# Two fused transformer blocks on one core: six seams of the schedule re-laid at once

## Chip, cores and metric

The kernel runs on one core of one Trainium2 chip. The metric is the device time of one execution in microseconds (us), taken as the median of several runs. All times below are of the kernel before the change.

## Reference, cut to what matters

The input `x` is 1024 tokens by 1024 features, float32. Two blocks follow each other.

```python
def first_block(x, ...):
    h = rmsnorm(x, norm_g)                       # x * rsqrt(mean(x^2)) * g
    q, k, v, z_att, gb, gc, u, z_conv, g_att, g_conv = split(h @ w_in)
    att = chunked_rel_attention(q, k, v, rel_bias)         # 8 heads of 64
    y_att = (att * silu(z_att)) @ w_att_out
    y_conv = (gb * causal_conv3(gc * u) * silu(z_conv)) @ w_conv_out
    x = x + (sigmoid(g_att) * y_att + sigmoid(g_conv) * y_conv) @ w_out
    return rmsnorm(x, final_norm_g)

def second_block(h, mem, ...):
    hn = rmsnorm(h, g_mix)
    q_a, k_a, v_a, q_i, k_i, w_i, q_b, k_b, v_b = split(hn @ w_in_2)
    # index scores of 4 heads -> the 256 best keys of each query -> attention A over these
    # attention B: softmax(q1 k1) - lam * softmax(q2 k2), 4 heads, causal
    h = h + concat(out_a, out_b) @ w_out_2
    h = h + softmax(q k_mem) v_mem @ w_xo         # cross attention, 256 memory rows, 4 heads
    a, gate = split(rmsnorm(h, g_ffn) @ w_ffn_in)
    return h + (gelu(causal_conv3(a)) * gate) @ w_ffn_out  # 2816 wide
```

## The kernel before, in words

Matrices lie feature-major in SBUF as tiles of 128 partitions by 1024 columns. Each float32 operand is cut into a high and a low part by `split` (ScalarE writes `hi` at L130, VectorE writes `lo` = x - hi at L133), and a product of two such operands is three matmuls on TensorE, hi by hi, lo by hi and hi by lo (`mm3`, every matmul at L204). Weights come through `w` or `parts`: a load on SyncE's queue into a raw tile `wr`, then `wh` (ScalarE) and `wl` (VectorE). Finished tiles go back to HBM through `dspill` (a DMA issued by GpSimd, L174).

The work goes through stages that follow each other on TensorE:

- start: `x_load` loads the eight tiles of x, cuts them, and `qk_start` begins the first projections with k outermost; the first weights are whole 128x1024 tiles, and the vectors of gains (`gvec`), of biases (`bvec`) and the positions are loaded on ScalarE's queue.
- attention of the first block, then `gates`: for j = 0 to 3 two x tiles are normalised (`normed`), turned into `operands` for the seven-product scheme of the later projections, and the attention output projection (`wao`) runs into two S tiles of PSUM, which are then evicted in halves through `s2` and `s3`. For x tiles 4 to 7, `normed` scales on ScalarE and multiplies by the broadcast norm R on GpSimd (L1554); for tiles 0 to 3 it is one instruction on VectorE (L136).
- `mixer` of the second block: projections are made in groups of 196 or 256 columns for all eight token tiles (`tok_group`). The first group (196 columns: index key, shared key, shared value, index weights) takes two S tiles, its keys go through `rope` and are transposed (L874) to KI and KA, then follows the group of index queries (`w2i`, QI, transposes at L888), then the index scores. The 31 counting steps of the search for each row's 256th best score (`topk_step`) are woven into the groups that follow: three tiles are counted on ScalarE (Sign into `jka`, L130), three on VectorE, and VectorE then moves the threshold C (L136). The groups come in the order qb, kb, v, qa, two of each. `diff_prep` loads Q and K of a head pair and transposes them (L1163); it stands between the two qa groups.
- attention B and A, the cross attention's memory side and the cross attention itself (`cross`): for each of four heads, `cross_q` of the next head is woven into `cross_att` of this one; the last head has nothing to weave in. Then the output projection (`wxo`) in the order of tiles 0, 4, 1, 5, 2, 6, 3, 7 with `dense_full`, and `operands` of the feed-forward.
- feed-forward: 22 rounds of seven products P1 to P7 on half matrices (`product`), with `left_x` and `left_y` making the left operands. Round 0 (`begin(0)` and what follows) also sums the squares (`col_sums`, L204 into A), and broadcasts the norm (`put_R`).

PSUM has two S tiles of 1024 columns, two T tiles of 512 and one each of A and D. Inside stretches marked manual on TensorE its order is the order of the code; elsewhere a scheduler sets the order of each engine's instructions when the program is built. On the chip each engine takes its instructions in that order and stops at the first whose inputs are not there.

## Time and profile before

| what | value |
|---|---|
| runs shown, median of 3 (lowest to highest) | 2587.79 us (2441.83 to 12579.39) |
| the profiled execution's own time | 2432.4 us |
| its span | 2430.6 us |
| mean granted TensorE clock | 0.983 of full |

The three runs lie far apart. The rows below come from the profiled execution, so its own time is the one that they add up to; it is 9.4 us under the lowest of the three. The span is the time from the first to the last instruction that the profiler saw. Engines are PE (TensorE), PEld (its weight loads), DVE (VectorE), ACT (ScalarE), POOL (GpSimd), SP (SyncE). A timeline row reads: start in us, duration in us, engine, line, operation, output <- inputs with shapes, and in brackets how long the engine had stood idle before it and what released it.

### The profile page before, as it was taken

How to read it: one execution, taken by the hardware profiler on the slowest of the kernel's cores; microseconds unless marked ns; L12 is line 12 of the kernel's file. 1: busy time of each engine (PE TensorE's matmuls, PEld its weight loads, DVE VectorE, ACT ScalarE, POOL GpSimd, SP SyncE). 2: the span in 40 equal slices, each digit the busy share in tenths (PEclk: the TensorE clock that was granted, in tenths of full speed). 3: DMA queues.
4: the chain of work that ended last, by engine and by line, in shares of the span. 5: the costliest groups of instructions: out<-in, count | busy, mean ns of one | idle time of the engine just before them, and what ended most of it. 6: DMA issues, size and time to landing. Idle time of an engine off the chain costs nothing. (4 is left out here: it accounts for less than half of the span.)

```text
span 2430.6 us, 32666 instructions
## 1 busy us (share of the span) xinstructions
PE 2332.1 (96%) x12324; PEld 1975.2 (81%) x12324; DVE 1628.9 (67%) x2664; ACT 1230.8 (51%) x2064; POOL 240.8 (10%) x386
## 2 busy tenths in 40 slices
PE   8999999999999899978798999999999999999999
PEld 7887878888888899977686877887778888888887
DVE  5476786777565568668868875345678888774433
ACT  4455654444424346777676764344444554453231
POOL 0000020111101114231111110000000000000000
PEclk9999999999999899999899999999999999999999
DMA  4323265767648443346563225112322222225554
GB/s 143 102 68 115 72 224 218 271 222 253 230 166 340 152 122 117 127 121 209 181 202 104 84 73 196 65 64 92 121 78 79 79 87 83 88 85 177 186 172 145
DMA packets 111134, 347.24 MB, mean 143 GB/s; under 512 B 13568, under 2 KB 19072, under 8 KB 110976
## 3 DMA queue, kind: packets, MB, share of 16 engines
q1 hardware_dynamic: 84960, 252.11, 31.7%
q0 software_dynamic: 25584, 92.81, 10.0%
q8 instruction: 97, 1.59, 0.3%
q14 instruction: 61, 0.50, 0.1%
q10 hardware_dynamic: 432, 0.23, 0.1%
HBM read 223.46 MB, written 100.14 MB: 133 GB/s over the span
## 5 line engine op out<-in xcount | busy, mean ns | idle before, releaser
L204 PE MATMUL S<-U,wh 128*128 128x512 f32 x1792 | 582.7, 392 | 16.9 <-ACT U L130 8.5
L204 PEld LDWEIGHTS S<-U,wh 128*128 128x128 f32 x1792 | 338.2, 189 | 90.8 <-ACT U L130 8.5
L204 PE MATMUL S<-U,wl 128*128 128x512 f32 x896 | 350.9, 392 | 1.8 <-DVE wl L133 1.8
L204 PE MATMUL D<-U,wh 128*128 128x512 f32 x816 | 284.0, 400 | 0.7 <-ACT wh L130 0.4
L204 PE MATMUL S<-U,U 128*128 128x256 f32 (+6 forms) x1040 | 216.3, 334 | 13.5 <-DVE st L516 10.8
L204 PE MATMUL S<-U,PT 128*128 128x512 f32 x912 | 224.9, 395 | 0.9 <-ACT jkd L130 0.7
L130 ACT ACTIVATE wh<-wr 128x1024 fp32r<-128x1024 f32 (+1 forms) x89 | 87.4, 982 | 266.0 <-PE D L204 171.6
L204 PEld LDWEIGHTS S<-U,PT 128*128 128x128 f32 x912 | 171.0, 188 | 42.3 <-ACT jkd L130 1.7
L204 PEld LDWEIGHTS S<-U,wl 128*128 128x128 f32 x896 | 169.3, 189 | 39.2 <-DVE wl L133 3.2
L133 DVE TENSOR_TENSOR wl<-wr,wh 128x1024 fp32r<-128x1024 f32 (+1 forms) x89 | 101.6, 1142 | 148.0 <-ACT wh L130 148.0
L204 PEld LDWEIGHTS S<-U,U 128*128 128x128 f32 x1040 | 158.6, 197 | 29.5 <-DVE st L516 13.0
L204 PEld LDWEIGHTS D<-U,wh 128*128 128x128 f32 x816 | 153.1, 189 | 30.5 <-DVE U L133 1.1
L204 PE MATMUL D<-U,wl 128*128 128x512 f32 x408 | 162.3, 398 | 0.4 <-DVE wl L133 0.4
L204 PE MATMUL T<-U,wh 128*128 128x512 f32 x480 | 161.1, 390 | 0.0
L130 ACT ACTIVATE P<-P,st 128x640 f32<-128x640 f32 (+7 forms) x168 | 124.0, 739 | 39.6 <-DVE st L516 37.4
L204 PE MATMUL S<-wh,U 128*128 128x256 f32 x768 | 142.0, 287 | 0.0
L130 ACT ACTIVATE PT<-T 128x512 fp32r<-128x512 f32 (+4 forms) x208 | 110.9, 545 | 56.0 <-PE T L523 45.9
L174 POOL DMA_DIRECT2D sp<-P x102 | 54.3, 533 | 806.8 <-DVE P L133 549.5
L133 DVE TENSOR_TENSOR PT<-U,PT 128x1024 fp32r<-128x1024 f32 x74 | 67.8, 955 | 98.6 <-PE S L204 97.5
L133 DVE TENSOR_TENSOR P<-P,P 128x1024 f32<-128x1024 f32 (+3 forms) x105 | 119.7, 1148 | 18.6 <-ACT P L130 18.4
L133 DVE TENSOR_TENSOR U<-U,U 128x512 f32<-128x512 f32 (+3 forms) x146 | 114.8, 802 | 21.5 <-ACT U L130 20.8
L130 ACT ACTIVATE P<-P 128x1024 f32<-128x1024 f32 (+2 forms) x105 | 101.5, 968 | 47.8 <-DVE P L133 21.6
(303 smaller groups left out, 4754.4 us busy)
## 6 DMA issues: line engine op xcount, KB each, us to landing
sp<-P POOLq DMA_DIRECT2D x102, 512.0 KB, 3.5
U<-sp SPq DMA_DIRECT2D x93, 512.0 KB, 4.6
sp<-U POOLq DMA_DIRECT2D x69, 512.0 KB, 3.9
P<-sp SPq DMA_DIRECT2D x56, 512.0 KB, 4.5
U<-in_wf SPq DMA_DIRECT2D x43, 512.0 KB, 3.5
U<-in_w SPq DMA_DIRECT2D x30, 512.0 KB, 4.2
U<-U SPq DMA_DIRECT2D x116, 128.0 KB, 2.4
wh<-sp SPq DMA_DIRECT2D x24, 512.0 KB, 3.6
```

Source lines behind the costliest of these rows:

```text
L130: return self.nc.scalar.activation(out, in_, f, **kw)
L133: return self.nc.vector.tensor_tensor(out, a, b, op=op)
L174: self.nc.gpsimd.dma_start(dt, src)
L204: self.last = self.nc.tensor.matmul(out, l, r, start=start, stop=stop, skip_group_check=True)
```

## The change

Six places are changed.

1. First loads: the first two weight tiles come as a piece of 128 columns and the rest (`start_weights`), x tile 0 comes and is cut in two halves, and `bvec` and the positions move to SyncE's queue behind the x tiles.
2. `gates`: `normed` is the VectorE instruction for all eight tiles; the first `wao` group runs k = 0, k = 1, then k = 2 and 3 of one S tile and of the other.
3. First mixer group: the 196-column group goes into one S tile, D and A; `rope` writes into one U tile; the transposes of KI and KA come behind the 192 matmuls of the `w2i` group, which runs in two halves of the tokens; the column sums of the norm use T.
4. Order of the groups: qb, kb, qa, v; `diff_prep` stands behind the first v group.
5. `cross`: while the last head is made, the first output tile of `wxo` is begun in D and A from the parts that are there (`begun`), k = 0 to 5, and 6 and 7 behind it.
6. Entry of the feed-forward: the left operands of round 0 are made during the last `wxo` tile, four additions of them on GpSimd; the operands of tile 7 are made half by half (`last_operands`); the column sums stand behind P7 and the two halves of `put_R` apart, around P4.

```diff
 x_load
-            x = self.load(self.big("U"), self.I["xT"][k])
+            if k == 0:
+                next(ws[0][1])
+                for c in (slice(0, 512), slice(512, 1024)):
+                    self.load(x[:, c], self.I["xT"][k][:, c])
+                next(ws[1][1])
...
 first block
-        w = [self.w(I["w1"][0])]
-        hn = self.x_load(lambda: w.append(self.w(I["w1"][4], tag="P")))
+        w = [self.start_weights(z) for z in range(2)]
+        hn = self.x_load(w)
+        self.load(self.bvec, I["bv"].to_broadcast([128, NBV]))
+        self.load(self.posi, I["pos"])
...
 gates
         def normed(x, k):
-            if k < 4:
-                self.stt(x, x, self.gv("norm", k), R, OP.mult, OP.mult)
-            else:
-                self.act(x, x, scale=self.gv("norm", k))
-                nc.gpsimd.tensor_tensor(x, x, R, op=OP.mult)
+            self.stt(x, x, self.gv("norm", k), R, OP.mult, OP.mult)
...
-                for k in range(4):
-                    for z in range(2):
+                for ks in ((0,), (1,), (2, 3)):
+                    for z, k in [(z, k) for z in range(2) for k in ks]:
...
 tok_group
-        if small:
+        if small == "SDA":
+            b = [self.t("S", [128, 1024])] + [self.t(x, [128, 512]) for x in "DA"]
...
+        if halves:
+            order = [(kh, 4 * q + z, range(4)) for q in range(2) for kh in range(2) for z in range(4)]
...
 mixer, first group
-        for t0, nt, ps in self.tok_group(None, hn2, 196, ws=ws, mid={(2, 0): self.rms1, (2, 3): self.rms2}):
+        for t0, nt, ps in self.tok_group(None, hn2, 196, ws=ws, small="SDA", mid={(2, 0): self.rms1, (2, 3): self.rms2}):
...
+        QI = [self.big("U", F32R) for _ in range(4)]
+        ws = ahead()
+        views = self.tok_group(None, hn2, 256, ws=ws, halves=True)
+        for K, ko in zip((KI, KA), kos):
+            for half in range(2):
                 T = self.t("T", [128, 512])
                 for t in range(4):
-                    nc.tensor.transpose(T[0:64, t * 128:t * 128 + 128], ko[:, t, 0], self.ident)
+                    nc.tensor.transpose(T[0:64, t * 128:t * 128 + 128], ko[:, half * 4 + t], self.ident)
...
 mixer, order of the groups
-        for name, dest in (("qb", QB), ("kb", KB)):
+        for name, dest in (("qb", QB), ("kb", KB), ("qa", QA)):
...
             par += 1
+            if g == 0:
+                qk0 = self.diff_prep(0, QB[0], KB[0])
         VB[1] = [self.dspill(x) for x in VB[1]]
-        tab = self.rope_tab("qa")
-        rope_group("qa", QA, 0, tab)
-        qk0 = self.diff_prep(0, QB[0], KB[0])
-        rope_group("qa", QA, 1, tab)
...
 cross
+        def begun(ks):
+            if not part:
+                part.append(self.w(I["wxo"][0]))
+                part.extend(self.t(x, [128, 512]) for x in "DA")
+            for k in ks:
+                parts(k + 1)
...
+                    self.mm3(part[1 + half], part[0][0][:, c], part[0][1][:, c], res[k][0][:, sl], res[k][1][:, sl],
+                             k == 0, k == 7)
+                yield 1360
         for h in range(4):
-            fill = self.cross_q(h + 1, self.hn3, qs) if h < 3 else iter(())
-            drain(weave(self.cross_att(h, *qs[h], out), fill, 2.2))
+            fill = self.cross_q(h + 1, self.hn3, qs) if h < 3 else begun(range(6))
+            drain(weave(self.cross_att(h, *qs[h], out), fill, 2.2 if h < 3 else 0.6))
             drain(fill)
+        drain(begun(range(6, 8)))
...
                 wh, wl = self.w(I["wxo"][d])
+                self.left_x(0, I["wf1"][22], "wr")
+                self.left = self.left_y(0, I["wf1"][0], "P", True)
+                next(self.left)
...
+                last = self.last_operands(xg[3], x, ps)
+                self.B[3] = dict([next(last)])
...
 left_y(early=True)
+        tt = (lambda o, a, b, op: self.nc.gpsimd.tensor_tensor(o, a, b, op=op)) if early else self.tt
+        tt(s12[:, h[0]], y[:, h[0]], y[:, h[1]], OP.add)
+        tt(s12[:, h[1]], s12[:, h[0]], x[:, h[0]], OP.subtract)
+        if early:
+            tt(s4, x[:, h[1]], s12[:, h[1]], OP.subtract)
+            tt(y[:, h[0]], x[:, h[0]], y[:, h[0]], OP.subtract)
...
 feed-forward, round 0
-            if f == 0:
-                norm.append(self.mean_rsqrt(self.col_sums(R, 8), 8, 1.0 / 1024))
             self.product(c, A, "P6", False)
...
             if f == 0:
-                self.put_R(norm[0])
-            self.tt(a[:, h[1]], a[:, h[1]], R[:, h[1]], OP.mult)
+                norm.append(self.mean_rsqrt(self.col_sums(R, 8), 8, 1.0 / 1024))
+            else:
+                self.tt(a[:, h[1]], a[:, h[1]], R[:, h[1]], OP.mult)
             nxt = following()
+            if f == 0:
+                self.put_R(norm[0], (1,))
+                self.tt(a[:, h[1]], a[:, h[1]], R[:, h[1]], OP.mult)
             self.product(c, A, "P4", False)
+            if f == 0:
+                self.put_R(norm[0], (0,))
```

How the instructions stand is shown at three places. The first is TensorE between the first mixer group and the `w2i` group. Before, the four transposes of the first index keys (line L874) follow the last matmul of the 196-column group (S_7045) directly, ahead of the `w2i` group (S_7409):

```order
L204 MATMUL S_7045<-U_6989,U_6995 128x196
L204 MATMUL S_7045<-U_6990,U_6994 128x196
L874 MATMUL T_7291<-ident_69,P_7279 64x128 x4
L204 MATMUL S_7409<-wh_7034,U_6415 128x256
L204 MATMUL S_7409<-wh_7034,U_6416 128x256
```

Now the same transposes (L917, out of the U tile that `rope` wrote) stand at the end of the `w2i` group, behind its second S tile S_7393, and are followed by matmuls of the next group into D:

```order
L204 MATMUL S_7393<-wh_7046,U_7000 128x256
L204 MATMUL S_7393<-wl_7047,U_6999 128x256
L917 MATMUL T_7586<-ident_67,U_7037 64x128 x4
L917 MATMUL T_7595<-ident_67,U_7037 64x128 x4
L204 MATMUL D_7938<-U_7384,U_6420 128x256
L204 MATMUL D_7938<-U_7384,U_6421 128x256
```

So 192 matmuls (96 into each of S_7392 and S_7393) moved ahead of the transposes. The second place is TensorE at the head preparation of attention B. Before, the first transposes of Q (L1163) follow the last matmul of the first qa group, whose last tile is T_9656, and the second qa group (S_10025) follows them:

```order
L204 MATMUL T_9656<-U_9390,U_6995 128x256
L204 MATMUL T_9656<-U_9391,U_6994 128x256
L1163 MATMUL T_9975<-ident_69,U_9973 128x128 x4
L204 MATMUL S_10025<-wh_9645,U_6415 128x256
L204 MATMUL S_10025<-wh_9645,U_6416 128x256
```

Now the first v group stands there (last tile T_9723), and the transposes (L1202) come eight matmuls into the second v group (S_10064), two of them together:

```order
L204 MATMUL S_10064<-wl_9713,U_6504 128x256
L204 MATMUL S_10064<-wh_9712,U_6592 128x256
L204 MATMUL S_10064<-wh_9712,U_6593 128x256
L1202 MATMUL T_10012<-ident_67,U_10010 128x128 x4
L1202 MATMUL T_10023<-ident_67,U_10010 128x128 x4
L204 MATMUL S_10064<-wl_9713,U_6592 128x256
```

The transposes moved by eight matmuls, from behind a qa group to behind a v group. What ScalarE does for that v group's tiles is the third place; the rows that read D, A and T are the scaled copies of the group's tiles, `jka` are the counts of the search, three to a step:

```order
L130 ACTIVATE jka_111,cnt_7897<-U_7698,C_7895 128x768
L130 ACTIVATE jka_111,cnt_7897<-U_7699,C_7895 128x896
L130 ACTIVATE U_9710<-A_9721,r_7198 128x256 x2
L130 ACTIVATE jka_111,cnt_7897<-U_7700,C_7895 128x1024
L130 ACTIVATE jka_111,cnt_7897<-U_7698,C_7895 128x768
L130 ACTIVATE U_9711<-T_9722,r_7198 128x256
L130 ACTIVATE jka_111,cnt_7897<-U_7699,C_7895 128x896
L130 ACTIVATE U_9711<-T_9722,r_7198 128x256
L130 ACTIVATE jka_111,cnt_7897<-U_7700,C_7895 128x1024
L130 ACTIVATE U_9711<-T_9723,r_7198 128x256 x2
L130 ACTIVATE jka_111,cnt_7897<-U_7698,C_7895 128x768
L130 ACTIVATE U_10004<-T_10012 128x512
```

Before, at the same place, the copies of the qa group's tiles and the counts alternate in the same way:

```order
L130 ACTIVATE jka_113,cnt_7872<-U_7673,C_7870 128x768
L130 ACTIVATE P_9907<-T_9655,r_7191 128x256
L130 ACTIVATE jka_113,cnt_7872<-U_7674,C_7870 128x896
L130 ACTIVATE P_9907<-T_9655,r_7191 128x256
L130 ACTIVATE jka_113,cnt_7872<-U_7675,C_7870 128x1024
L130 ACTIVATE PT_9912<-P_9907 128x512
L130 ACTIVATE P_9935<-T_9656,r_7191 128x256
L130 ACTIVATE jka_113,cnt_7872<-U_7673,C_7870 128x768
L130 ACTIVATE P_9935<-T_9656,r_7191 128x256
```

The copies moved from the rope path (P and PT tiles) to plain copies into U, and the counts still stand between them.

## Rows read from the trace of the kernel before

**Rows 1.** Page, part 1: busy time, share of the span, instructions of each engine.

```profile
PE 2332.1 (96%) x12324; PEld 1975.2 (81%) x12324; DVE 1628.9 (67%) x2664; ACT 1230.8 (51%) x2064; POOL 240.8 (10%) x386
```

**Rows 2.** Windows: stretch, us, busy PE, PEld, DVE, ACT, POOL, clock, DMA, GB/s.

```profile
0.00:45.00 45.00, 34.59 (x160) 29.09 (x161) 26.56 (x36) 25.46 (x27) 3.50 (x41) 0.92 0.41 146
320.00:362.00 42.00, 37.62 (x155) 29.94 (x154) 35.67 (x40) 27.64 (x37) 14.65 (x4) 0.96 0.54 189
805.00:885.00 80.00, 72.42 (x557) 70.55 (x556) 36.00 (x85) 22.71 (x52) 11.95 (x17) 0.91 0.43 132
1045.00:1100.00 55.00, 35.86 (x274) 34.85 (x273) 41.07 (x106) 37.86 (x75) 22.19 (x31) 0.85 0.52 161
1100.00:1340.00 240.00, 209.79 (x1395) 182.40 (x1395) 190.49 (x482) 167.93 (x456) 33.67 (x44) 0.96 0.54 166
1640.00:1665.00 25.00, 19.76 (x96) 16.35 (x96) 13.24 (x20) 13.91 (x30) 1.64 (x1) 0.80 0.11 39
1750.00:1780.00 30.00, 24.14 (x105) 19.06 (x105) 19.37 (x25) 14.13 (x17) 2.56 (x2) 0.89 0.29 99
```

**Rows 3.** Timeline, the first 19 us.

```profile
4.93 0.17 DVE L133 TENSOR_TENSOR fgm<-gvec 128x8 f32<-128x8 f32 x1 [3.89 <-DMA gvec<-in_gv]
7.29 1.15 ACT L130 ACTIVATE U<-U,gvec 128x1024 fp32r<-128x1024 f32 x1 [1.49 <-DMA U<-in_xT]
8.49 0.79 PE L204 MATMUL S<-U,wh 128*128 128x512 f32 x1 [8.49 <-ACT U L130]
10.06 8.81 ACT L130 ACTIVATE U<-U,gvec 128x1024 fp32r<-128x1024 f32 x7 [0.20 <-DMA U<-in_xT]
```

**Rows 4.** Timeline of the gates' entry, 318 to 358 us.

```profile
320.65 1.28 DVE L136 SCALAR_TENSOR_TENSOR P<-P,gvec,R 128x1024 f32<-128x1024 f32 x1
327.36 2.39 POOL L1554 TENSOR_TENSOR P<-P,R 128x1024 f32<-128x1024 f32 x1 [3.18 <-ACT P L130]
328.26 2.57 DVE L133 TENSOR_TENSOR wl<-wr,wh 128x1024 fp32r<-128x1024 f32 x1 [1.01 <-ACT wh L130]
330.75 1.21 DVE L133 TENSOR_TENSOR U<-PT,U 128x1024 fp32r<-128x1024 f32 x1
349.47 6.39 POOL L1554 TENSOR_TENSOR P<-P,R 128x1024 f32<-128x1024 f32 x1 [8.64 <-issue]
357.97 0.50 PE L204 MATMUL S<-U,wh 128*128 128x512 f32 x1 [2.17 <-ACT jkd L130]
```

**Rows 5.** Timeline of the first mixer group, TensorE, 840 to 883 us.

```profile
840.14 1.06 PE L874 MATMUL T<-ident,P 128*64 128x128 f32 x4 [4.32 <-DVE P L133]
882.79 2.08 PE L204 MATMUL S<-U,U 128*128 128x512 f32 x8 [0.39 <-DMA U<-PT]
```

**Rows 6.** Timeline of attention B's entry, 1045 to 1100 us.

```profile
1046.04 0.94 ACT L130 ACTIVATE jka<-U,C 128x768 int8<-128x768 f32 x1 [0.56 <-DVE C L136]
1050.08 0.94 ACT L130 ACTIVATE jka<-U,C 128x768 int8<-128x768 f32 x1 [0.56 <-DVE C L136]
1060.55 1.12 PE L1163 MATMUL T<-ident,U 128*128 128x128 f32 x4 [10.80 <-ACT P L130]
1078.87 1.06 PE L1163 MATMUL T<-ident,U 128*128 128x128 f32 x8 [2.59 <-DMA U<-sp]
1096.69 0.58 PE L204 MATMUL D<-wh,U 128*128 128x256 f32 x1 [4.82 <-DMA U<-sp]
1099.06 0.40 ACT L130 ACTIVATE P<-P,st 128x128 f32<-128x128 f32 x1 [2.70 <-DVE st L516]
```

**Rows 7.** Timeline of the last cross head, 1640 to 1650 us.

```profile
1640.49 0.17 DVE L133 TENSOR_TENSOR st<-A,r 128x8 f32<-128x8 f32 x1 [1.96 <-PE A L204]
1648.32 1.94 PE L523 MATMUL T<-ident,P 128*128 128x128 f32 x8 [3.21 <-DVE P L133]
```

**Rows 8.** Timeline of the feed-forward's entry, TensorE, 1755 to 1762 us.

```profile
1755.99 1.95 PE L204 MATMUL A<-ones,R 128*128 128x1 f32 x16 [1.24 <-DVE R L133]
1761.35 0.80 PE L204 MATMUL S<-U,wh 128*128 128x512 f32 x1 [3.41 <-ACT wh L130]
```

More of the change, by code (lines that the diff above doesn't have):

```diff
@@ L527, in transposed, with put_R @@
         return PT
-    def put_R(self, r):
-        for half in range(2):
+    def put_R(self, r, halves=(0, 1)):
+        for half in halves:
             ps = self.t("T", [128, 512])
@@ L549, in x_load @@
             if k == 0:
-                between()
+                for z, n in ((1, 1), (0, 2), (1, 2)):
+                    for _ in range(n):
+                        next(ws[z][1], None)
         self.gate0 = his[GATE]
@@ L854, in mixer @@
         VA = self.big("U", F32R)
-        todo = [("w2i",)] + [(n, g) for n in ("w2q", "w2k", "w2v", "w2a") for g in range(2)]
+        todo = [("w2i",)] + [(n, g) for n in ("w2q", "w2k", "w2a", "w2v") for g in range(2)]
         ready = [self.first]
@@ L862, in ahead @@
             return ready.pop(0)
+        kos = self.big("U").rearrange("p (z t d) -> p z t d", z=2, t=8)
+        kos = [kos[:, z] for z in range(2)]
         ws = ahead()
[L865 removed]
+        for t0, nt, ps in self.tok_group(None, hn2, 196, ws=ws, small="SDA", mid={(2, 0): self.rms1, (2, 3): self.rms2}):
             self.v_split(ps[:, :, 128:192], t0, nt, VA.rearrange("p (t s d) -> p t s d", t=8, s=2)[:, t0:t0 + nt])
@@ L879, in mixer @@
         kas, vas = [self.dspill(k.bitcast(F32)) for k in KA], self.dspill(VA.bitcast(F32))
-        QI = [self.big("U", F32R) for _ in range(4)]
-        ws = ahead()
-        for t0, nt, ps in self.tok_group(None, hn2, 256, ws=ws):
+        for t0, nt, ps in views:
             qo = self.big("P")
@@ L1466, in rest @@
         def rest():
-            self.B[3].update(ops[3])
+            self.B[3].update(last)
             self.add_sq(acc, x, False)
@@ L1496, in operands, with last_operands, pair, put @@
                 yield n, (hi[:, c], lo[:, c])
+    def last_operands(self, x, y, ps):
+        h = [slice(0, 512), slice(512, 1024)]
+        u = self.big("U", F32R)
+        self.split(u[:, h[0]], u[:, h[1]], x[:, h[0]])
+        yield "11", (u[:, h[0]], u[:, h[1]])
+        def pair():
+            return self.big("U", F32R), self.big("U", F32R)
+        def put(v, hl, c, name):
+            self.split(hl[0][:, c], hl[1][:, c], v[:, c])
+            return name, (hl[0][:, c], hl[1][:, c])
+        z, zs = self.big("P"), pair()
+        for c in h:
+            self.tt(y[:, c], y[:, c], ps[:, c], OP.add)
+            self.act(z[:, c], y[:, c], scale=self.gv("ffn", 7))
+        yield put(z, zs, h[0], "21")
+        one, two = self.big("PT"), self.big("PT")
+        self.tt(one[:, h[0]], x[:, h[1]], x[:, h[0]], OP.subtract)
+        self.tt(two[:, h[0]], z[:, h[1]], one[:, h[0]], OP.subtract)
+        twos = pair()
+        yield put(two, twos, h[0], "T2")
+        ones = pair()
+        yield put(one, ones, h[0], "T1")
+        self.tt(one[:, h[1]], z[:, h[1]], x[:, h[1]], OP.subtract)
+        yield put(one, ones, h[1], "T3")
+        self.tt(two[:, h[1]], z[:, h[0]], two[:, h[0]], OP.subtract)
+        yield put(two, twos, h[1], "N4")
+        yield put(z, zs, h[1], "22")
     def left_x(self, f, ap, tag="U"):
@@ L1777, in ffn @@
             self.rest()
-            drain(self.left_y(0, I["wf1"][0]))
+            drain(self.left)
             for f in range(22):
```

107 lines of the change are left out of this document (68 added, 39 removed).

## Prediction

> **What bounds the kernel now.** I read the busy times first: TensorE works 2332.1 of 2430.6 us [rows 1], so all its waits together are 98.5 us, and an edit that takes no matmul away can gain only from these waits and from matmuls that run at a lowered clock. Then I read the windows of the places that the six edits touch, where the idle time is the stretch less the busy time of TensorE [rows 2]: start 45.00 − 34.59 = 10.4; gates 42.00 − 37.62 = 4.4; first mixer group 7.6; entry of attention B 19.1; last cross head 5.2; feed-forward entry 5.9. Together 52.6 us. The attention stretch behind the entry, 1100 to 1340, holds another 30.2, which no edit aims at. The clock column of the same rows is below 1.00 in each: if I charge the busy time of each with what is missing from full clock (34.59 × 0.08, 37.62 × 0.04, 72.42 × 0.09, 35.86 × 0.15, 19.76 × 0.20, 24.14 × 0.11), I get 2.8 + 1.5 + 6.5 + 5.4 + 4.0 + 2.7 = 22.9 us. That is an upper bound, since part of the lowered clock belongs to waits that stay. So the six places hold at most 52.6 + 22.9 = 75.5 us, 3.1% of the time; what each edit gets of it is read from the timelines, by asking what ends the wait and what is late next.
>
> The sums are made against the profiled execution's own 2432.4 us (span 2430.6 and 1.8 around it). The median of the runs shown, 2587.79, comes from three values far apart; the lowest, 2441.83, is 9.4 above the profiled one. I take the profiled one as the kernel's time.
>
> **First loads in pieces.** TensorE's first matmul is at 8.49; it waits for the cut of x tile 0 on ScalarE, which takes 1.15 from 7.29, after waiting for the tile's load [rows 3]. Ahead of it on SyncE's queue stood a whole weight tile; now a piece of 128 columns and half of x stand there (64 and 256 KB, where 1024 KB came before). The gain vector that the cut needs is there at 4.93 [rows 3], and that DMA is not moved, so a half-wide cut of some 0.6 (half of 1.15) can start at about 5.1 and the first matmul at about 5.7: 2.8 earlier. What is late next is x tile 1, cut from 10.06 on [rows 3]; twelve matmuls of 512 columns from 5.7 at 0.43 (512 columns at the lower of the clock's levels, 1.2 GHz) end near 10.8, and its cut ends at about 11.2 (10.06 + 1.15), with its low part behind it: a wait of about 0.7 comes back. 2.8 − 0.7 = 2.1, I take 2; bounds 1 and 3. The bias and position loads move past the x tiles on SyncE's queue; the rows show no use of them before the start's end, so I cost that at nothing, within the lower bound.
>
> **Gate norms on VectorE.** Removed: four GpSimd multiplies (2.39 to 6.39, in all 14.65 in this stretch) and four ScalarE scalings. Added: four VectorE instructions like the one of 1.28 at 320.65 [rows 4], 5.1 us. VectorE is busy 35.67 of 42.00 [rows 2], so 40.8 must fit. It gets something back: while GpSimd multiplies from 327.36 to 329.75, a VectorE subtraction begun at 328.26 takes 2.57, where the same size takes 1.21 at 330.75; 1.4 saved. The GpSimd multiply that runs among back-to-back VectorE work takes 6.39 [rows 4]. So VectorE ends at about 39.4 of 42 us: it still fits, with little room. The waits (idle 4.4, one of them the 2.17 at 357.97) are for what the S tiles' eviction and the late operands release, and the reordered first group finishes its first S tile 12 matmuls earlier. All 4.4 and some of the 1.5 of clock give 5 to 6; I take 5. Bounds 2 (VectorE late by up to 2 at the end, and no clock back) and 6.5.
>
> The same rows weigh a rule. The Trainium skill, page "SBUF — State Buffer", section "Who interferes with whom", says that a VectorE instruction with two SBUF inputs contends with a GpSimd instruction that reads SBUF, that the lock is on their one shared port pair, and that issue order decides who waits. The trace agrees: 329.75 + 1.21 = 330.96, and the subtraction ended at 330.83. By that rule this edit gains also what the waiting cost, but the four GpSimd additions of the feed-forward's entry, below, would bring the waiting back there.
>
> **First mixer group.** Before, TensorE stops 4.32 at 840.14 for the key transposes, because `rope` of 196-column tiles on VectorE is not finished; now 192 matmuls stand in between, and VectorE, busy 36.00 of 80.00 [rows 2], has the time. No matmul is added, and the work ahead of the index scores is the same, so these start earlier by the waits that go: the 7.6 of the stretch less the 0.39 in front of the scores [rows 5], 7.2, which puts the scores near 875.5 where 882.79 stood. I take 7 (waits alone, with any clock gained set against a new small wait). Low: the second half of `w2i` must still be roped and transposed before the scores with less behind it; if the last transposes wait 4, 3 is left. High: 9, with 2 of the 6.5 of clock.
>
> **Value groups last.** Before, three waits make 10.80 + 2.59 + 4.82 = 18.2 of the 19.1 [rows 6]. The first is for a T tile of PSUM that ScalarE copies late, because the copies stand among the counts of the search. After the change the transposes need T tiles that are released by the copies of T_9722 and T_9723, and between the group's first copies and these stand eight counts, 2.67 steps. A step takes 1050.08 − 1046.04 = 4.04 [rows 6], so 10.8; the eight matmuls ahead cover 1.7 (256 columns each, 0.21 at 1.2 GHz). 9.1 us of wait remain there. The other two waits are for loads from HBM (Q and K of the pair, and the memory weights); I let half of 7.4 remain, 3.7. So 18.2 − 9.1 − 3.7 = 5.4. Against that stands the end of this stretch: the first exponential at 1099.06 follows counting steps whose number (17) the edit does not change, and those are a chain of ScalarE and VectorE, not of TensorE. Filling work that TensorE does earlier is then missing behind it. I take 4. Bounds: 13 (most waits and the 5.4 of clock go) and −4 (the chain is untouched, and the memory work moved ahead is missing as fill in 1100 to 1340).
>
> **Last cross head filled.** From the row sums at 1640.49 to the transposes at 1648.32 the softmax of the last head takes 7.8, of which TensorE waits 3.21 [rows 7]; the stretch idles 5.2 and its clock is 0.80. Now the 48 matmuls of the first output tile are there to be spread, and in the built order 12 of them stand between the row sums and the last scores: at 0.21 to 0.43 each (512 columns at either clock) 2.6 to 5.1 us beside a wait of 3.2. But the parts of the output have to be cut first by ScalarE and VectorE, which are on the chain too, and later waits of the head have less fill. I leave 2 of the 5.2 and half of the 4.0 of clock: 3.2 + 2 = 5. Bounds 1 and 8. The matmuls are the same ones, so nothing is added; the eviction of D and A is two half-wide additions instead of one.
>
> **Feed-forward entry.** Waits 1.24 for the squares and 3.41 for `wh` [rows 8], 5.9 in all, and 2.7 of clock (the matmul at 1761.35 took 0.80). The left operands now come during the last projection, and column sums and norm move behind P7. What is late next are the right operands: `last_operands` is a chain of splits on ScalarE and subtractions on VectorE, half by half, that cannot start before the last projection ends. I let 3.5 of the wait and 2 of the clock stay: 8.6 − 5.5 = 3. GpSimd's four additions lie beside the last projection; at half of 2.39 each they are 4.8 us, covered. If they hold up VectorE as at 328.26, two collisions of 1.4 come on the path, and with the splits unchanged the gain is −1, the lower bound; the upper is 7.
>
> **Sum.** 2 + 5 + 7 + 4 + 5 + 3 = 26, and 2432.4 − 26 = 2406. All lower bounds: 1 + 2 + 3 − 4 + 1 − 1 = 2, so 2430; all upper bounds: 3 + 6.5 + 9 + 13 + 8 + 7 = 46.5, so 2386.
>
> **Rivals.**
> *The chains take it back.* Attention B's entry is bound by the counting steps and the feed-forward's by the splits, so these two give nothing or a little less: with 0 and −1, and 3 for the cross head, 2 + 5 + 7 + 0 + 3 − 1 = 16 and 2416. For it speaks that ScalarE's counts stand between the copies just as before; against it, that two of the three waits at the entry were for loads.
> *Nearly all of it goes.* The waits vanish where fill stands: 2386 by the upper bounds. Against it, each wait has a chain behind it that is not shortened. Only here does the time fall by over 2%.
> *Slower, through the attention stretch.* The work that fills attention B's entry now is missing in 1100 to 1340, where ScalarE and VectorE (167.93 and 190.49 of 240.00) feed TensorE. If the waits there multiply so that the clock falls from 0.96 to the 0.80 of the cross head's stretch, its 209.79 us become 209.79 × 0.96 / 0.80 = 251.7, 42 more; with the other five edits' 22, 2432.4 − 22 + 42 = 2452. It decides from a clock of about 0.87 on (209.79 × 0.96 / 0.87 = 231.5, the 22 gone). Against it: only 18 us of waits could move there, and 30.2 of them cost it 0.04 so far.
> *The change does not do what it says.* The fills could stand in the queue at places where they don't meet the waits, at the cross head above all; then the mixer's and the gates' gain alone remain: 2 + 5 + 7 = 14, 2418; this lies beside the first rival.
>
> **Chances.** The forecast 0.52; the chains take it back, or fills miss, 0.30; nearly all goes 0.12; slower than before 0.06. A measurement of this kernel can tell about 2% from no change, 48.6 us. Faster by that needs under 2384, beyond the upper bounds: half of the third case and a little for runs that scatter, 0.09; slower by that needs over 2481, beyond the slower case: 0.03; the rest is within. The range goes from 2388, leaving out the best of the third case, to 2438, which takes in the lower bounds' 2430 and most of the 9.4 by which a run can lie above the profiled one.
>
> **What would show it.** In the new profile: first matmul near 5.7; no GpSimd multiply in the gates, and VectorE done before TensorE needs its weights; index scores some 14 us earlier than before (2 + 5 + 7); at the first head transposes behind the v group one wait of 8 to 10 us, and the first exponential some 18 us earlier than 1099.06; transposes of the last cross head with a wait under 2; at the feed-forward's entry waits of 3 to 4 in all. The prediction is wrong if the transposes wait longer than the 10.80 of before, if the stretch behind the entry idles over 40, or if the four additions on GpSimd last over 3 us and VectorE's instructions beside them grow with them.

## Result and the profile after

The changed kernel takes 2409.69 us (median of four executions, 2408.14 to 2414.48), a ratio of 0.9887 to the kernel before, 95% interval 0.9863 to 0.9912: some 27 us less. Two of the three runs of before that were shown first had been disturbed; its later executions lie between 2430.27 and 2445.14, so the profiled 2432.4 is near their lower end. Against that one execution the gain is 22.7 us. Run again beside it on two other occasions, the same changed kernel gave 0.9890 (0.9870 to 0.9909) and 0.9891 (0.9873 to 0.9908). The profiled execution after is 2414.48, the slowest of its four, 17.9 under the profiled one of before; where two executions of one kernel come to differ by 6 us is seen in the table below.

Page, part 1, of the changed kernel, against [rows 1]:

```profile
PE 2335.0 (97%) x12324; PEld 1977.2 (82%) x12324; DVE 1632.2 (68%) x2682; ACT 1228.5 (51%) x2068; POOL 234.7 (10%) x388
```

TensorE does the same 12324 matmuls. The windows that answer to [rows 2], moved along with what each place had gained (columns as there: us, busy PE, PEld, DVE, ACT, POOL, clock, DMA, GB/s):

```profile
0.00:45.00 45.00, 36.66 (x158) 30.29 (x159) 26.80 (x38) 25.92 (x30) 3.50 (x41) 0.89 0.42 146
317.00:359.00 42.00, 41.25 (x179) 33.51 (x179) 40.89 (x47) 25.16 (x34) 0.00 (x0) 1.00 0.69 239
801.00:881.00 80.00, 75.23 (x572) 73.26 (x570) 38.06 (x98) 24.36 (x54) 12.53 (x19) 0.91 0.43 132
1039.00:1094.00 55.00, 43.87 (x320) 42.32 (x319) 35.89 (x116) 49.65 (x103) 4.06 (x14) 0.84 0.61 190
1094.00:1334.00 240.00, 207.94 (x1349) 180.11 (x1349) 187.07 (x467) 164.62 (x444) 33.07 (x43) 0.94 0.52 157
1633.00:1658.00 25.00, 22.95 (x128) 19.19 (x127) 13.97 (x21) 14.75 (x31) 1.64 (x1) 1.00 0.19 64
1734.00:1764.00 30.00, 27.22 (x121) 21.26 (x120) 24.67 (x35) 15.85 (x23) 2.60 (x2) 0.94 0.27 88
```

A window less the busy time of TensorE is what it waits. The gates wait 0.75 and the cross head 2.05 (4.4 and 5.2 before), both at the full clock. The start waits 2 us less, at a lower clock. The mixer still waits 4.8, attention B's entry 11.1 (7.6 and 19.1 before), and the stretch behind it 32.1 where it was 30.2. No experiment below undoes the filling of the last cross head; that its matmuls now stand in the waits of [rows 7] is read from TensorE's timeline, in which these waits are left:

```profile
1641.49 1.07 PE L529 MATMUL T<-ident,P 128*128 128x128 f32 x8 [0.66 <-DVE P L133]
1648.24 0.50 PE L204 MATMUL D<-U,wh 128*128 128x512 f32 x1 [1.40 <-ACT U L130]
```

Since the numbered order of the matmuls is the same in all kernels outside the changed places, the time between two equally numbered matmuls measures a place by itself. The table gives, from the trace of one execution of each kernel, the time of matmul 241 (end of the start), and the times from matmul 1741 to 2041 (gates), 3841 to 4621 (mixer to behind the index scores), 5701 to 7441 (attention B's entry to the end of attention), 8821 to 9121 (cross) and 9301 to 9661 (feed-forward's entry). The first four rows are the two kernels of the forecast and two repeats of the changed one; the other names are the experiments below.

```
kernel        start   gates   mixer  attention  cross  feed-forward
before        54.70   73.52  119.60   306.31    65.98   88.49
after         54.86   68.02  118.18   306.19    59.05   84.97
again         55.39   67.96  115.09   309.64    59.05   85.00
again2        57.21   67.75  112.62   306.14    59.05   85.00
no_start      54.67   67.95  114.78   305.63    59.03   84.96
no_mix        54.83   67.99  120.66   304.49    59.03   84.95
no_val        55.61   67.35  116.55   310.42    59.02   84.93
gpsimd_mul    57.19   72.41  115.76   304.74    59.03   84.97
start3        57.65   67.32  117.28   302.89    59.03   84.99
qi_queue      54.70   67.33  113.94   306.67    59.02   84.96
sums_early    57.47   67.35  115.13   307.23    59.02   92.03
left_dve      56.87   67.40  116.40   303.65    59.02   83.99
qi_pool       54.15   67.86  112.72   305.44    59.00   84.97
q_free        53.55   67.44  112.02   317.69    59.04   84.95
best          54.80   67.43  113.13   302.19    59.04   84.00
best2         55.97   67.69  111.42   318.26    59.03   83.98
best3         55.01   67.28  112.52   305.39    59.05   84.00
```

Three columns repeat within 0.8 us wherever their code is the same (gates, cross, feed-forward); start, mixer and attention scatter by 4 to 7 for identical code. So the pair before and after alone would have misjudged the mixer (1.4 won) and attention (0.1 won); with all kernels that have the new code there unaltered, the mixer is 115.8 on average (after, again, again2, no_start, no_val, gpsimd_mul, start3, sums_early, left_dve) against 119.6 and 120.7 with the old, and attention 305.4 (the thirteen without no_val, q_free and best2) against 306.3 and 310.4. The mixer's two old values lie above all nine new ones. Those of attention don't: the thirteen go from 302.2 to 309.6, with the old 306.3 among them.

### The profile page after: what moved, and what is told of

Read it like the earlier page. It is cut to its first block, busy times and chain, and to the rows that moved or that the text cites. A ratio compares the mean times of both kernels' runs of the same rounds, so it can differ in the third digit from the quotient of the medians.

```text
span 2412.7 us, 32693 instructions
## 1 busy us (share of the span) xinstructions
PE 2335.0 (97%) x12324; PEld 1977.2 (82%) x12324; DVE 1632.2 (68%) x2682; ACT 1228.5 (51%) x2068; POOL 234.7 (10%) x388
## 5 line engine op out<-in xcount | busy, mean ns | idle before, releaser
L204 PE MATMUL S<-U,wh 128*128 128x512 f32 x1768 | 575.3, 392 | 7.6 <-ACT U L130 6.0
L204 PEld LDWEIGHTS S<-U,wh 128*128 128x128 f32 x1768 | 333.3, 189 | 80.2 <-ACT U L130 6.4
L204 PE MATMUL D<-U,wh 128*128 128x512 f32 x832 | 290.5, 400 | 3.8 <-ACT U L130 2.6
L204 PE MATMUL S<-U,U 128*128 128x256 f32 (+6 forms) x944 | 207.6, 342 | 18.8 <-DVE st L522 12.7
L130 ACT ACTIVATE wh<-wr 128x1024 fp32r<-128x1024 f32 (+2 forms) x90 | 87.6, 973 | 263.4 <-PE D L204 171.5
L133 DVE TENSOR_TENSOR wl<-wr,wh 128x1024 fp32r<-128x1024 f32 (+2 forms) x90 | 100.4, 1116 | 148.6 <-ACT wh L130 148.5
L204 PEld LDWEIGHTS S<-U,U 128*128 128x128 f32 x944 | 148.9, 199 | 36.2 <-DVE st L522 14.7
L204 PE MATMUL A<-U,wh 128*128 128x512 f32 x384 | 131.4, 390 | 0.0
```

What stands on the lines that cost most here:

```text
L130: return self.nc.scalar.activation(out, in_, f, **kw)
L133: return self.nc.vector.tensor_tensor(out, a, b, op=op)
L204: self.last = self.nc.tensor.matmul(out, l, r, start=start, stop=stop, skip_group_check=True)
```

## Experiments

**The first loads** (no_start): change 1 undone. Of each edit the lines that matter are shown; three dots stand for the rest.

```diff
-        w = [self.start_weights(z) for z in range(2)]
-        hn = self.x_load(w)
+        w = [self.w(I["w1"][0])]
+        hn = self.x_load(lambda: w.append(self.w(I["w1"][4], tag="P")))
...
```

> The changed kernel with the first loads as before (whole weight tiles, x tile 0 whole, biases and positions on ScalarE's queue). Theory 1, what is won at the first matmul is given back to x tile 1 and to the lowered clock: first matmul back near 8.5 us, but the start's matmuls end within 0.5 us of the changed kernel's. Theory 2, the forecast's term: they end 2 us later.

Theory 1 holds for this pair: first matmul at 8.54 instead of 4.84, end of the start 54.67 against 54.86. The timeline of TensorE in the changed kernel shows what was given back, and its window from 12 to 24 us the clock:

```profile
4.84 0.79 PE L204 MATMUL S<-U,wh 128*128 128x512 f32 x1 [4.84 <-ACT U L130]
10.95 0.50 PE L204 MATMUL S<-U,wh 128*128 128x512 f32 x1 [1.14 <-ACT U L130]
12.27 1.08 PE L204 MATMUL S<-U,wh 128*128 128x512 f32 x2 [0.59 <-DVE U L136]
...
12.00:24.00 12.00, 11.73 (x45) 9.52 (x46) 10.25 (x9) 11.36 (x11) 0.00 (x0) 0.86 0.59 229
```

and the window of the kernel without the edit:

```profile
12.00:24.00 12.00, 12.00 (x54) 9.91 (x54) 11.04 (x10) 11.36 (x12) 0.00 (x0) 1.00 0.56 214
```

From 4.84 on TensorE works at the lower clock (five matmuls of 512 columns from 5.85 to 7.99, 0.43 each), waits 1.14 and 0.59 for the next x tile, and then is granted 0.86 where the old start has 1.00: 45 matmuls against 54 in the same 12 us. The two waits alone would leave 3.7 − 1.7 = 2.0 of the earlier start; with the clock nothing is left. This is one execution of each. In others of the changed kernel's start the clock from 12 to 24 was 1.00 (again, again2 and q_free), the waits before 13 us were longer or shorter, and the start ended anywhere from 53.55 to 57.47, against 54.67 to 55.97 with the old loads. So no gain was shown; which of waits and clock takes the lead back differs from one execution to the next.

An attempt at the cause of these waits (start3): `pieces` in three parts, x tile 1 asked for ahead of the last.

```diff
-            for c in (slice(0, 128), slice(128, 1024)):
+            for c in (slice(0, 128), slice(128, 256), slice(256, 1024)):
...
```

> The changed kernel with the first two weight tiles in three pieces (128, 128 and 768 columns), so that x tile 1 is asked for ahead of the 768. Theory 1, what the start gave back was a wait for x tile 1 and the lowered clock behind it: both waits (1.14 and 0.59 at 10 to 12 us) go, and the start's matmuls end 1.5 to 3 us earlier than the changed kernel's. Theory 2, the lowered clock comes back wherever TensorE starts early, wait or no wait: under 1 us.

Neither. The wait was 2.16 (at 12.13), x tile 1 was cut from 10.93 on instead of 9.75, and the start ended at 57.65. But the same wait scatters as far with unaltered loads: 0.52 in again, 0.88 in again2, 2.30 in sums_early and, the longest, in no_mix:

```profile
12.11 0.80 PE L204 MATMUL S<-U,wh 128*128 128x512 f32 x1 [2.45 <-ACT U L130]
```

So one execution of start3 decides nothing about the pieces.

**The gates** (gpsimd_mul): `normed` as before, the new order of the first group kept.

```diff
-            self.stt(x, x, self.gv("norm", k), R, OP.mult, OP.mult)
+            if k < 4:
+                self.stt(x, x, self.gv("norm", k), R, OP.mult, OP.mult)
+            else:
+                self.act(x, x, scale=self.gv("norm", k))
+                nc.gpsimd.tensor_tensor(x, x, R, op=OP.mult)
```

> The changed kernel with the norms of x tiles 4 to 7 on ScalarE and GpSimd again, but the new order of the first output group. Theory 1, the late GpSimd products and the instructions that they hold up made the waits: the gates' entry is 4 to 6 us longer, with VectorE instructions of over 2 us beside the GpSimd ones. Theory 2, the order of the first group made them go: under 2 us longer.

Theory 1: 72.41 against 67.3 to 68.0, so 4.4 to 5.1 come with the GpSimd products. The remaining 1.1 to the 73.52 of before is left for the order of the first group, which no run undid by itself. From its timelines (PE, POOL, DVE):

```profile
333.01 0.50 PE L204 MATMUL S<-U,wh 128*128 128x512 f32 x1 [0.91 <-ACT jkd L130]
334.08 2.64 POOL L1658 TENSOR_TENSOR P<-P,R 128x1024 f32<-128x1024 f32 x1 [2.69 <-ACT P L130]
356.44 3.45 POOL L1658 TENSOR_TENSOR P<-P,R 128x1024 f32<-128x1024 f32 x1 [8.63 <-ACT P L130]
331.42 0.69 DVE L133 TENSOR_TENSOR PT<-P,P 128x512 f32<-128x512 f32 x1 [2.29 <-POOL P L1658]
334.98 2.82 DVE L133 TENSOR_TENSOR wl<-wr,wh 128x1024 fp32r<-128x1024 f32 x1 [0.53 <-ACT wh L130]
357.68 2.77 DVE L133 TENSOR_TENSOR PT<-P 128x512 f32<-128x512 f32 x1
```

VectorE's 2.82 beside the product at 334.08 answers to the 2.57 against 1.21 of [rows 4], and the 128x512 instruction of 2.77 beside the product at 356.44 takes 0.69 elsewhere. VectorE also waits 2.29 for a product that comes late (331.42). How much is collision and how much lateness was not separated.

**The mixer's first group** (no_mix): the group in two S tiles, keys transposed ahead of `w2i`, as before.

```diff
-        for t0, nt, ps in self.tok_group(None, hn2, 196, ws=ws, small="SDA", mid={(2, 0): self.rms1, (2, 3): self.rms2}):
+        for t0, nt, ps in self.tok_group(None, hn2, 196, ws=ws, mid={(2, 0): self.rms1, (2, 3): self.rms2}):
...
-        views = self.tok_group(None, hn2, 256, ws=ws, halves=True)
+        for t0, nt, ps in self.tok_group(None, hn2, 256, ws=ws):
```

> The changed kernel with the first mixer group and its key transposes as before. Theory 1, the index scores are held by SyncE's queue of small QI copies, so the new order gave only 1.4 us: the stretch from the 196-column group to behind the index scores is 1 to 2 us longer, the wait for keys (4 us) is back and the wait of 3.6 in front of the scores is gone. Theory 2, the forecast's term: 7 us longer.

The wait for the keys is back, and the stretch is 120.66: 2.5 longer than in the profiled execution after, 4.9 than the mean of 115.8. So the term is between the theories, and 120.66 lies above the 118.18 that is the longest of the nine. Its wait:

```profile
835.87 1.06 PE L911 MATMUL T<-ident,P 128*64 128x128 f32 x4 [4.31 <-DVE P L133]
```

In the changed kernel the wait stands in front of the index scores, on SyncE's small copies of QI (timeline of PE and SP's queue):

```profile
876.16 3.60 PE L204 MATMUL S<-U,U 128*128 128x512 f32 x8 [3.59 <-DMA U<-PT]
...
861.95 1.71 SPq L502 DMA_DIRECT2D U<-U  x2
866.92 1.47 SPq L504 DMA_DIRECT2D U<-PT  x2
868.51 0.52 SPq L502 DMA_DIRECT2D U<-U  x1
870.81 0.60 SPq L502 DMA_DIRECT2D U<-U  x1
873.79 1.10 SPq L504 DMA_DIRECT2D U<-PT  x2
```

Each set of queries takes three copies; the third (L504) overwrites what the first (L502) reads, so it waits until that has landed, and the second half's copies stand behind it in the queue. The scores come 11.25 after the last transposes (864.91), where it was 882.79 − 875.07 = 7.7 before, and the first matmuls of the scores then take 3.60 for eight, against 2.08 in [rows 5]. A second thing moved there and was not tested: the key copies that GpSimd issues (L921) and two spills, issued from 842 to 860 before, now lie from 857.81 to 867.5, beside the copies of QI.

Half of the copies on ScalarE's queue (qi_queue):

```diff
-                self.move_q(QI[2 * pr:2 * pr + 2], T, slice(t0 * 128, t0 * 128 + 512))
+                self.move_q(QI[2 * pr:2 * pr + 2], T, slice(t0 * 128, t0 * 128 + 512), eng=(nc.sync, nc.scalar)[pr])
...
```

> The changed kernel with the six small QI copies of the second pair of index heads issued on ScalarE's queue, the other six on SyncE's. Theory 1, the index scores are held by twelve copies issued one after the other on SyncE's queue (12.9 us): the last is issued some 5 us earlier, the wait of 3.59 in front of the scores falls under 1, and the mixer's stretch is 3 to 5 us shorter. Theory 2, the copies are held by the DMA engines or the scores by the chain of ScalarE and VectorE: under 1 us.

The stretch took 113.94, which identical code reaches too (112.62 to 118.18), so neither theory is shown by it. The wait in front of the scores is 0.35, but 2.40 for VectorE stand ahead of it, since ScalarE itself now stood behind the third copy (5.68 idle at 863.85), and from the last transposes to the scores it is 11.2 us as in the changed kernel. The third copy alone on GpSimd's queue (qi_pool):

```diff
-        dma(f(hi[64:]), f(lo[:64]))
+        (last or dma)(f(hi[64:]), f(lo[:64]))
...
-                self.move_q(QI[2 * pr:2 * pr + 2], T, slice(t0 * 128, t0 * 128 + 512))
+                self.move_q(QI[2 * pr:2 * pr + 2], T, slice(t0 * 128, t0 * 128 + 512), last=nc.gpsimd.dma_start)
```

> The changed kernel with only the last of each three QI copies on GpSimd's queue. Theory 1, SyncE's queue stood still behind that copy: the other eight are issued within 8 us of each other, the wait in front of the index scores falls from 3.59 to under 1, the mixer's stretch is 2 to 4 us shorter than the 118.18 of the changed kernel. Theory 2, the copies' own landing times are the bound: the wait stays over 2.

```profile
865.13 0.52 SPq L502 DMA_DIRECT2D U<-U  x1
869.62 0.52 POOL L504 DMA_DIRECT2D U<-PT  x1 [1.60 <-DMA U<-U]
873.45 2.08 PE L204 MATMUL S<-U,U 128*128 128x512 f32 x8 [3.69 <-DMA U<-PT]
```

Theory 2: SyncE's queue is free at 866.3, and still the wait is 3.69; the copies' landings follow each other, 4.5 us from the issue of the first to that of the third and 3.8 from there to the scores. The eight matmuls behind the same wait took 2.08 here, so the slow ones of the changed kernel don't belong to every such wait. The stretch is shorter all the same, 112.72, within the scatter of the changed kernel (again2 has 112.62). Then the order of the copies was taken away (q_free): the high parts in a tile of their own, their lower half once more by ScalarE in place.

```diff
-        self.split(hi, lo, src, scale)
+        lo, hi = x[:, :n], x[:, n:2 * n]
+        self.split(hi, lo, src, scale)
+        self.act(q[0:64], src[0:64], **({} if scale is None else {"scale": scale}))
...
-        dma(f(hi[64:]), f(lo[:64]))
+        dma(f(q[64:]), f(lo[:64]))
```

> The changed kernel with the high parts of each query set written to a tile of their own and, for the lower 64 partitions, once more by ScalarE in place, so that none of the three copies waits for another (this holds for the index queries, the head preparation of attention B and the queries of attention A; each set costs one ScalarE instruction of 0.6 more). Theory 1, two landings one after the other held the scores: the way from the last index query transposes to the first scores, 11.3 us in the changed kernel, falls to 8 or less, the wait of 3.6 to under 1, the mixer's stretch to 113 to 115 us. Theory 2, the copies' number or the spills beside them hold it: over 10 us, the wait stays over 2.

```profile
868.74 2.09 PE L204 MATMUL S<-U,U 128*128 128x512 f32 x8 [1.86 <-DMA U<-PT]
```

The way from the last transposes (859.43) fell to 9.3 us and the wait to 1.86, the stretch to 112.02: between the theories. So the two landings are part of it. What holds the rest is open: the twelve copies take 10.9 us to issue on one queue, but best3 below, with half of its independent copies on ScalarE's queue, has 11.1 us from the last transposes to the scores, with waits of 2.16 for ScalarE and 1.78 for the copies. The same instruction put into the head preparations of attention B and the queries of attention A cost 11 us there (317.69).

**The value groups** (no_val): the order qb, kb, v, qa, head preparation between the qa groups.

```diff
-        for name, dest in (("qb", QB), ("kb", KB), ("qa", QA)):
+        for name, dest in (("qb", QB), ("kb", KB)):
...
+        rope_group("qa", QA, 0, tab)
+        qk0 = self.diff_prep(0, QB[0], KB[0])
+        rope_group("qa", QA, 1, tab)
...
```

> The changed kernel with the groups in the order qb, kb, v, qa and the head preparation between the two qa groups, as before. Theory 1, the entry is given back before the first head ends: the stretch from the last kb group to the end of attention B and A is within 1.5 us of the changed kernel's, though the first exponential comes 3 to 5 us later. Theory 2, the forecast's term: 4 us longer.

Its first transposes and first exponential,

```profile
1055.13 1.11 PE L1204 MATMUL T<-ident,U 128*128 128x128 f32 x4 [11.44 <-ACT P L130]
...
1093.72 0.40 ACT L130 ACTIVATE P<-P,st 128x128 f32<-128x128 f32 x1 [2.70 <-DVE st L522]
```

and those of the changed kernel, with what follows (PE and ACT):

```profile
1049.90 1.12 PE L1202 MATMUL T<-ident,U 128*128 128x128 f32 x4 [5.20 <-ACT U L130]
1083.27 0.55 PE L204 MATMUL D<-wh,U 128*128 128x256 f32 x1 [2.66 <-DMA U<-sp]
1088.90 0.40 ACT L130 ACTIVATE P<-P,st 128x128 f32<-128x128 f32 x1 [0.56 <-DVE C L136]
1102.93 1.10 PE L1202 MATMUL T<-ident,U 128*128 128x128 f32 x8 [1.21 <-DMA U<-sp]
1107.44 1.21 PE L204 MATMUL S<-U,U 128*128 128x448 f32 x4 [2.72 <-DVE st L522]
```

The entry itself is won: 5.20 for 11.44 and, against the groups' start (matmul 5701 at 1035.4 in both), the exponential 4.8 us earlier. Behind it the first head waits 6.0 us up to matmul 6121, most for the next head's Q (1102.93) and for VectorE (1107.44), where no_val waits 3.3: matmul 6121 starts at 1117.35 with the change and at 1117.94 without. The edit reorders matmuls 5769 to 6126 and none behind. From 5701 to 6121 the thirteen kernels with the new order take 81.3 on average (79.65 to 83.13), no_val 82.57 and before 81.85, so 0.5 to 1.2 us are left of the edit there. Behind 6121 the order is the same, and identical code takes 221.0 to 228.3 (no_val 227.84, before 224.47). The whole attention, 310.42 and 306.31 with the old order against 305.4, therefore shows no gain clear of the scatter: up to matmul 6121 theory 1 holds, behind it nothing is decided.

**The feed-forward's entry** (sums_early): the column sums behind P2 and both halves of `put_R` ahead of P4, all else as changed.

```diff
             self.tt(g[:, h[0]], o, s1, OP.add)
+            if f == 0:
+                norm.append(self.mean_rsqrt(self.col_sums(R, 8), 8, 1.0 / 1024))
...
             if f == 0:
-                norm.append(self.mean_rsqrt(self.col_sums(R, 8), 8, 1.0 / 1024))
+                self.put_R(norm[0])
...
```

> The changed kernel with the column sums of the feed-forward's first round behind P2 and both halves of the norm's broadcast ahead of P4, as before; the early left operands and the half-wise operands of tile 7 stay. Theory 1, the early operands made the 3.5 us at the feed-forward's entry: under 1 us longer. Theory 2, the moved sums did: a wait of 1 us or more for the squares is back and the entry is 1.5 to 3.5 us longer.

```profile
1752.72 3.58 PE L204 MATMUL A<-ones,R 128*128 128x1 f32 x16 [5.09 <-DVE R L133]
```

Theory 2, and by more than it said: 7.1 longer, 3.5 longer than before the change. With the operands made early and the sums not moved, TensorE waits 5.09 for the squares, where it waited 1.24 [rows 8]. What the moved sums are worth without the early operands was not run. GpSimd's additions on VectorE instead (left_dve):

```diff
-        tt = (lambda o, a, b, op: self.nc.gpsimd.tensor_tensor(o, a, b, op=op)) if early else self.tt
+        tt = self.tt
```

> The changed kernel with the four early additions of the left operands on VectorE instead of GpSimd. Theory 1, they lie beside the last projection, where VectorE has room: within 0.5 us at the entry, and the VectorE instructions that took 5.7 us for three beside GpSimd take 2.1. Theory 2, VectorE is what the entry waits for: 1 to 3 us longer.

Neither: 1.0 shorter, 83.99 (best, best2 and best3 repeat it). The collision is in the changed kernel's timelines (POOL and DVE):

```profile
1726.54 1.46 POOL L1617 TENSOR_TENSOR P<-P 128x512 f32<-128x512 f32 x1
1728.08 2.17 POOL L1617 TENSOR_TENSOR P<-P,wr 128x512 f32<-128x512 f32 x1
1730.21 1.75 POOL L1617 TENSOR_TENSOR P<-wr,P 128x512 f32<-128x512 f32 x1
1731.91 1.74 POOL L1617 TENSOR_TENSOR jkd<-wr,P 128x512 f32<-128x512 f32 x1
1729.01 5.72 DVE L133 TENSOR_TENSOR U<-P,U 128x512 fp32r<-128x512 f32 x3
```

where left_dve has 1.29 for two of this kind and no GpSimd work beside it:

```profile
1726.11 1.29 DVE L133 TENSOR_TENSOR U<-P,U 128x512 fp32r<-128x512 f32 x2
```

TensorE's waits that are left at the entry of the changed kernel:

```profile
1741.29 0.50 PE L204 MATMUL D<-U,wh 128*128 128x512 f32 x1 [1.22 <-ACT U L130]
1742.52 0.50 PE L204 MATMUL D<-U,wh 128*128 128x512 f32 x1 [0.50 <-DVE U L133]
1751.50 0.50 PE L204 MATMUL S<-U,wh 128*128 128x512 f32 x1 [0.93 <-ACT cs L130]
```

**The whole again, and versions from the findings.** again and again2 are the changed kernel unaltered; best leaves out the first loads' edit, with left_dve and qi_pool; best2 is q_free with the first two; best3 has independent copies for the index queries alone, half of them on ScalarE's queue.

> The changed kernel, unaltered, beside the kernel before on one chip. If the profiled pair's 18 us are the change's worth, the ratio is near 0.9926; if the mean over several executions is, which the single runs put near 27 us, near 0.989.

> The changed kernel without its edit of the first loads, with the four early additions on VectorE, and with the last of each three QI copies (the one that must wait until the first has landed) issued on GpSimd's queue, so that it does not hold SyncE's queue. From the runs so far each is worth about 1, 1 and 2 to 4 us: 4 to 6 us less than the changed kernel run beside it, near 0.9975 of it. If the gains lie within the scatter of the lowered clock instead, the two are within 2 us.

> q_free without the edit of the first loads and with the four early additions on VectorE. Theory 1: 4 to 8 us less than the changed kernel's 2409 to 2411, a ratio to the kernel before of 0.986 or 0.987. Theory 2: the same 0.989 as the changed kernel.

> The changed kernel once more, on the same chip as best3: 2408 to 2412, ratio 0.989.

> The changed kernel without the edit of the first loads, with the early additions on VectorE, and with independent copies for the index queries alone, half of them on ScalarE's queue. Theory 1: the wait in front of the scores is under 1, the mixer's stretch 109 to 112 us (118 and 115 in two executions of the changed kernel), the stretches of attention B and A as in the changed kernel; 5 to 8 us less than its 2410, ratio 0.986. Theory 2, what the mixer wins the counting steps behind it keep: the stretch from the last kb group to the end of attention grows by as much, ratio 0.989.

again 2411.41 us (0.9890), best beside it 2408.46 (0.9885, 0.9868 to 0.9902); best2 2421.79 (0.9937, 0.9919 to 0.9955); again2 2408.85 (0.9891), best3 beside it 2406.88 (0.9871, 0.9851 to 0.9891). best is 3 us ahead of again, less than the 4 to 6 expected; best2, behind both of its theories, loses in attention what q_free lost. best3 is 2 us ahead, with intervals that overlap; no version was shown to beat the changed kernel. best3's theory 1 failed in the wait (2.16 and 1.78 in place of under 1) and, at 112.52, in the stretch; its theory 2 isn't borne out either, since attention took 305.39, like the changed kernel's.

## Why the prediction was right, and where not

The forecast was 2406, 26 us under the profiled 2432.4; measured 2409.69, 22.7 under that execution and some 27 under the kernel before by the ratio, since before's executions have medians of 2433.73 to 2437.72 where nine or more were run. Taking the profiled execution for the kernel's time, and not the 2587.79, was right. That the sum came so near is in part luck: its terms miss on both sides and cancel. What failed are the step for the start, of which nothing came, and the way from the last transposes to the index scores, which was left at its old length; the gain at attention's entry is not shown.

The terms, forecast and measured by the table: start 2, measured −0.6 (55.0 on average without the edit, 55.6 with it, a difference within the scatter); gates 5, measured 5.5 to 6.2; mixer 7, measured 4.4; attention's entry 4, measured 3.0 against only two values of the old order, of which 0.5 to 1.2 lie where the order was changed; cross 5, measured 6.9; feed-forward 3, measured 3.5. Together 23, the 22.7 of the profiled execution.

- **Start: this step failed.** "a wait of about 0.7 comes back" measured 1.14 + 0.59 = 1.7, and the clock behind these waits, which the term put at nothing, fell to 0.86 from 12 to 24. The step had the early matmuls at the lower level, but not the return to it. Its first half held: the first matmul came even earlier than 5.7, at 4.84, since the gain vector was there at 3.12 and not at 4.93 (its load was not moved, but two others behind it on ScalarE's queue were). In other executions the lead went in other waits; in the mean nothing was left.
- **Gates: right**, step by step: no GpSimd product, no wait but 0.75 at 317.89, clock 1.00, VectorE at 40.89 of 42 (40.8 forecast without, 39.4 with what the collisions gave back). gpsimd_mul shows most of it to come with the GpSimd products; the part of the collisions alone is not shown. The first S tile is finished 6 matmuls earlier than before, not 12: it was 6 ahead of the group's end already.
- **Mixer: mechanism right, size off.** The 4.32 went. "these start earlier by the waits that go" priced the way from transposes to scores at what it was before, 7.7 us; it became 11.25, and the wait of 3.59 is new. The low end named this place, "if the last transposes wait 4, 3 is left", though through rope; the wait is for the copies of QI. The scores began 882.79 − 876.16 = 6.6 earlier, not 14.
- **Entry of attention B: mis-sized, and the gain is not shown.** One wait of 8 to 10 was forecast, 5.20 + 0.74 came, and the exponential was 10.2 earlier, not 18. "eight counts" were priced, 10.8 us; in the trace five stand between the copies of D (from 1041.76) and the release of the first T tile (1049.85), 8.1 us. That what is won is missing behind it, the reason for taking 4 of 5.4, is what matmul 6121 shows, and more of it went than the term allowed. The slower rival did not come: the stretch behind idles 32.1, clock 0.94.
- **Cross head: right**, under-sized. Transposes wait 0.66 (1.40 once more at 1648.24), and the clock is 1.00 in place of 0.80, of which half had been claimed.
- **Feed-forward: right in sum, not in its parts.** Waits of 1.22, 0.50 and 0.93 remain, 2.65 where 3 to 4 were forecast. Without the move of the sums, costed as one part among others, the early operands lose 3.5 us instead of winning as much (sums_early). GpSimd's additions were "covered", but one of the prediction's signs of being wrong came, if its 3 us are meant for the four together: they took 7.1 us in all and three VectorE instructions beside them 5.72, while the entry is 1.0 shorter without them (left_dve). That a VectorE instruction with two SBUF inputs contends with a GpSimd instruction that reads SBUF is the rule of the Trainium skill's page "SBUF — State Buffer", section "Who interferes with whom". The trace agrees: three such VectorE instructions take 5.72 beside GpSimd's additions, and two of them 1.29 without.

## What to carry to other kernels

When a wait is filled, price the whole way to the next consumer again: here, behind the filled wait, a new one of 3.59 stood 20 us later, in front of the next consumer. An engine that starts earlier need not end earlier: here 3.7 us of lead went into later waits and the lower clock behind them. And judge small edits by the time between two equally numbered instructions in many executions, not by one pair of spans; take the stretch no longer than the edit reaches, since what scatters behind it hides a microsecond.

## What was not expected of the hardware

Identical code took 112.62 to 118.18 us in the mixer's stretch. The granted clock goes along: in the window 800 to 886 it was 0.92 in the execution with 118.18, 0.94 in again (115.09) and 0.98 in again2 (112.62). What sets it in one execution and not in the next is not shown. Copies of 128 KB within SBUF that depend on each other took 4.5 and 3.8 us each from issue to the next step (qi_pool), against a median of 2.4 from issue to landing for the 116 copies of that size from U to U in the page of before.
